# The FFN weight blocks of a two-layer decoder: loads, high parts and low parts tied to one order on three queues

## The chip, the cores and the metric

The kernel runs on one core of one Trainium2 chip. A core has engines that run side by side, each with a queue of its own: TensorE (PE in the profile; PEld is its weight load), VectorE (DVE), ScalarE (ACT), GpSimd (POOL) and SyncE (SP), which here only issues DMA transfers. The metric is the device time of one execution in microseconds, as a median over runs.

## The reference: what is computed

Two layers work on 528 tokens (16 learned meta tokens and 512 real ones) of width 1024. Each layer has a mixer sub-layer (attention heads, a convolution group and a short gated convolution that read one projection) and an FFN sub-layer. The change touches the FFN alone:

```python
u = rms_norm(h, pre_g)
z = jnp.einsum("bld,df->blf", u, w_up)          # 1024 -> 2 * 2816
z = causal_depthwise_conv(z, conv_w)            # 3 taps along the tokens
g, up = jnp.split(z, 2, axis=-1)
y = jnp.einsum("blf,fd->bld", jax.nn.silu(g) * up, w_down)   # 2816 -> 1024
return h + rms_norm(y, post_g)
```

All of it is float32.

## The kernel before, in words

**Three products for one.** TensorE runs in its fast float32 format, which keeps fewer bits. So each operand is split in a high part (a rounded copy) and a low part (the rest), and a product is made of high by high, high by low and low by high. A weight block takes three steps before TensorE can use it: a load from memory into a `raw` tile (issued by SP), the high part by a copy with a cast on ACT (tile `whi`), and the low part by a subtraction on DVE (tile `wlo`).

**Blocks and their order.** `chunk_list` writes down all weight blocks in the order in which they are used. In the FFN the 22 column pairs f (a gate block and an up block of 1024 x 128 each) come in three parts of 8, 7 and 7; behind each part come eight blocks of the down projection. `next_w` takes the next block that is ready and has `prep_one` issue the three steps for blocks further on, so that two are ahead.

**Pairs with seven products.** For the f in `SEVEN` (15 to 20 in the first layer; 8 to 13 and 15 to 20 in the second) `seven_pair` uses a scheme of Strassen's kind: seven block products in the place of eight, on sums of weight blocks that other code has stored in `w_sum`. `prep_one` then makes four blocks of a pair: the gate block (g below; lines 646, 648, 649) and three parts "c", "b" and "d" (lines 630, 638, 639). `seven_pair` calls for them as g, c, b, d. The products run g, c, then the d of the pair before (kept back in `late_ups`), then b, g, c, b.

**Buffers.** g and c go to `whi` and `wlo`, three buffers each; b goes to `shi` and `slo`, one buffer each; d goes to the tiles of `y_pair(7)`, one buffer. `raw` has three buffers; in parts 1 and 2, while pairs with seven products are still to come, four places in the tile of h serve too (`spare_tile`), in a fixed round of seven, save while `down_sum` uses them.

**What sets the order of instructions.** In the mixers and at the ends of the sub-layers (`manual_schedule`) a planner in the kernel (`Flow`) writes the order out. Elsewhere, so in the bulk of the FFNs, a scheduler at build time sets the order on each engine: of the instructions that could start by its estimates it takes the one that was written first. An instruction that was written later can go ahead of an earlier one that has to wait for a buffer. `tc.issue_after(ins)` adds one rule: what is written inside it and runs on the same engine as `ins` is issued behind `ins`. It makes no wait between engines.

**Other users of these orders.** `last_load` and `last_low` hold the last load and the last subtraction. The copies of `sum_steps` and the reload of h at the end of the last pair are issued behind `last_load`; the steps of `down_sum` behind `last_low`. Before the change `last_load` isn't set by the loads of parts c, b and d. The down products' results are copied out of PSUM at line 2403 (part 0, ACT) and added at line 2405 (part 1, DVE).

Of the kernel before, what the change touches and what calls it, by code (L numbers as in the profile page):

```python
# [10 lines left out]
F32 = mybir.dt.float32  # L11
# [5 lines left out]
P = 128  # L17
# [100 lines left out]
def chunk_cols(c):  # L118
    return sum(n for _, n in c[4])
# [254 lines left out]
def stt_us(n):  # L374
    return 0.22 + 0.00102 * n
# [13 lines left out]
def tile_hybrid_trunk(ctx: ExitStack, tc: tile.TileContext, xT, wflat, pv_d, out):  # L389
    nc = tc.nc  # L390
# [3 lines left out]
    def T(pool, shape, dt, tag, bufs=None):  # L394
        uid[0] += 1
        kw = {} if bufs is None else {"bufs": bufs}
        return pool.tile(list(shape), dt, tag=tag, name=f"{tag}_{uid[0]}", **kw)
# [89 lines left out]
    def half_sl(hf):  # L487
        return slice(H * hf, H * (hf + 1))
# [15 lines left out]
    offs = []  # L504
# [15 lines left out]
    def flat_w(i):  # L520

        n = chunks[i][3] * chunk_cols(chunks[i])
        return wflat[offs[i]:offs[i] + P * n].rearrange("(p s) -> p s", p=P)
# [32 lines left out]
    def wtile(i, tag):  # L556
        if chunks[i][0] == "a_pw_w":
            if tag == "whi":
                pw_place[0] = pw_place[0]()
            n = chunks[i][3] * chunk_cols(chunks[i])  # L560
            return pw_place[0][:, :n] if tag == "whi" else pw_place[0][:, n:2 * n]
        return T(wx[0], [P, WCHUNK], F32R, tag) if i in wide else T(wp, [P, CHUNK], F32R, tag)

    parts, last_load, last_low = deque(), [None], [None]
    spare, n_raw = [None], [0]

    def spare_tile(j):
# [3 lines left out]
    def raw_tile():  # L571

        if spare[0] is not None and not in_spare[0]:
            j = (None, 0, None, 1, None, 2, 3)[n_raw[0] % 7]
            n_raw[0] += 1
            if j is not None:
                return spare_tile(j)
        return T(wp, [P, CHUNK], F32, "raw", 3)
# [39 lines left out]
    def prep_one():  # L618
        i = wpos[0]
        if i >= len(chunks):  # L620
            return
        if i in seven_up:
            if not parts:
                t = sums[seven_up[i]]
                parts.extend((("c", t[:, 1::2]), ("b", t[:, 0:3:2]), ("d", flat_w(i)[:, SB:])))
            kind, src = parts.popleft()
            wpos[0] += not parts
            raw = raw_tile()
            sz = SB if kind == "d" else 2 * SB
            nc.sync.dma_start(raw[:, :sz] if kind == "d" else raw[:, :sz].rearrange("p (e s) -> p e s", e=2),  # L630
                              src)
            if kind == "b":
                hi, lo = (T(tx[0], [P, 2 * SB], F32R, t) for t in ("shi", "slo"))
            elif kind == "c":
                hi, lo = (T(wp, [P, CHUNK], F32R, t) for t in ("whi", "wlo"))
            else:
                hi, lo = y_pair(max(PARTS) - 1)
            nc.scalar.copy(hi[:, :sz], raw[:, :sz])
            last_low[0] = nc.vector.tensor_sub(lo[:, :sz], raw[:, :sz], hi[:, :sz].bitcast(F32))
            ready.append((i, tuple(t[:, :sz].rearrange("p (k n) -> p k n", n=P) for t in (hi, lo))))  # L640
            return
        wpos[0] += 1
        kn, n = chunks[i][3], chunk_cols(chunks[i])
        sz = kn * n
        raw = raw_tile()
        last_load[0] = nc.sync.dma_start(raw[:, :sz], wflat[offs[i]:offs[i] + P * sz].rearrange("(p s) -> p s", p=P))
        hi, lo = wtile(i, "whi"), wtile(i, "wlo")
        nc.scalar.copy(hi[:, :sz], raw[:, :sz])  # L648
        last_low[0] = nc.vector.tensor_sub(lo[:, :sz], raw[:, :sz], hi[:, :sz].bitcast(F32))  # L649
        ready.append((i, tuple(t[:, :sz].rearrange("p (k n) -> p k n", n=n) for t in (hi, lo))))  # L650

    to_store = deque(i for i, c in enumerate(chunks) if c[1] == 1 and c[0] == "w_in" and MASK[sum(d[:2] == c[:2] for d in chunks[:i])] == "1")
# [21 lines left out]
    def prefetch(n):  # L674

        while wpos[0] < len(chunks):
            if wpos[0] not in wide and sum(i not in wide for i, _ in ready) >= n:
                return
            prep_one()
# [8 lines left out]
    def dve(us, fn, *after, **kw):  # L688
        return flow.op("dve", us, fn, after, **kw)
# [152 lines left out]
    def two(t):  # L842
        return t.rearrange("p (a b) -> p a b", a=2)
# [1172 lines left out]
    def y_pair(i):  # L2016
        t = T(ypool, [P, 2, L], F32R, f"y{i}")
        return t[:, 0], t[:, 1]
# [6 lines left out]
    with tc.tile_pool(name="pre", bufs=2, reuse_waits="tile") as sp, tc.manual_schedule(engines=every):  # L2025
# [13 lines left out]
        for k in range(KD):  # L2039
            hk, hi, lo, gc = h[:, k, :H], u_raw[0][k], u_raw[1][k], g0[:, k:k + 1]  # L2040
            c = act(act_us(H) + 0.06, lambda hk=hk, hi=hi, gc=gc: nc.scalar.activation(hi, hk, AF.Copy, scale=gc),
                    h_at[0, k - k % 2], prio=0)
            d = dve(stt_us(H), lambda hk=hk, hi=hi, lo=lo, gc=gc: nc.vector.scalar_tensor_tensor(
                lo, in0=hk, scalar=gc, in1=hi.bitcast(F32), op0=ALU.mult, op1=ALU.subtract), c, prio=0)
# [45 lines left out]
    for l in range(DEPTH):  # L2090
# [23 lines left out]
        with tc.tile_pool(name=f"fp{l}", bufs=2, reuse_waits="tile") as fp:  # L2114
# [223 lines left out]
            for part, nf in enumerate(PARTS):  # L2338
# [41 lines left out]
                if part < len(PARTS) - 1:  # L2380
# [3 lines left out]
                    for some in ((0, 1), *((m,) for m in range(2, KD))):  # L2384
# [12 lines left out]
                        for m, ps in zip(some, tiles):  # L2397
                            if final:
                                d, src = yp[:, m, t0:], ps[:, 0, :2 * fw]
                            else:  # L2400
                                d, src = two(yp[:, m, t0:]), ps[:, :, :fw]
# [7 lines left out]
                else:  # L2409
# [7 lines left out]
                    if not final:  # L2417
                        raw = list(zip(*[g[f0 + k] for k in range(nf)], y_pair(nf)))
                        raw = [[[t[:, half_sl(hf)] for t in ts] for ts in raw] if hf < 2 else None for hf in range(2)]
# [64 lines left out]
```

## Time and profile before

| | us |
|---|---|
| median of 3 runs | 1271.03 (1269.31 to 1271.58) |
| the profiled execution | 1270.68 |
| its span | 1269.0 |
| PE busy | 1249.8 (98%) |
| DVE busy | 920.9 (73%) |
| ACT busy | 705.2 (56%) |

The span is the time between the first and the last instruction of the profiled execution; its own time is a little longer. L646 is line 646 of the kernel. SPq is SP's DMA queue. In a row of waits stand the total, the count and the longest. In a timeline row stand the start and the length in us, the engine, the line, the operation and its tiles, and in square brackets how long the engine sat idle before it and who ended that.

### The profile page before, as it was taken

The page shows a single profiled execution, that of the slowest core. Times are in us where ns is not written, and L with a number is a line of the kernel's source. Part 1 is how long each engine was busy: PE and PEld are TensorE (multiplying, and loading weights), DVE is VectorE, ACT ScalarE, POOL GpSimd, SP SyncE. Part 2 cuts the span into 40 slices and gives each one's busy share as a digit, 9 for nine tenths or more (in the row PEclk, how much of TensorE's full clock was granted, in tenths as well). Part 3 has the DMA queues.
Part 4 walks back from the last instruction along what each step waited for, and adds up shares of the span by engine and source line. Part 5 has one row for each costly group of instructions (what it writes and reads, how often), then busy time and mean ns, then how long its engine had stood idle before and what let it go on. Part 6 is the DMA issues. An engine that isn't in the chain of part 4 may idle for free.

```text
span 1269.0 us, 24272 instructions
## 1 busy us (share of the span) xinstructions
PE 1249.8 (98%) x9590; PEld 1198.2 (94%) x9590; DVE 920.9 (73%) x1569; ACT 705.2 (56%) x1365; POOL 162.0 (13%) x343
## 2 busy tenths in 40 slices
PE   8999999999999999999999999999999999999997
PEld 8998898999999999999999988999999799979996
DVE  7887866589874665587688878656799748756954
ACT  7254576654444643476673545775554447526763
POOL 1324311001101100000003244110021000000000
PEclk9999999999999999999999999999999999999999
DMA  7257231726558634544552584547166655475611
GB/s 243 81 155 175 72 102 53 249 86 151 182 164 313 212 112 142 205 165 144 192 205 61 159 191 113 143 118 233 70 166 184 172 176 169 152 241 160 202 61 67
DMA packets 76146, 197.93 MB, mean 156 GB/s; under 512 B 8240, under 2 KB 18608, under 8 KB 75520
## 3 DMA queue, kind: packets, MB, share of 16 engines
q1 hardware_dynamic: 64048, 162.69, 40.0%
q0 software_dynamic: 11984, 33.69, 11.1%
q8 instruction: 75, 1.23, 0.4%
q14 instruction: 39, 0.32, 0.1%
HBM read 162.17 MB, written 44.30 MB: 163 GB/s over the span
## 4 chain that ended last, share of the span: by engine, by line
PE 66%; DVE 2%; ACT 1%; issue 0%; DMA 0%; POOL 0%; DVEq 0%; ACTq 0%
PE psum L833 45%; PE psum L2281 14%; PE psum L1403 2%; PE psum L1667 2%; PE psum L970 1%; PE psum L1633 1%; PE psum L1589 0%; DMA h<-w_sum 0%; DVE yp L1046 0%; PE psum L1733 0%; PE psum L1319 0%; DVE h L1056 0%; POOL dm L1604 0%; DVE ulo L1064 0%; DVE wlo L649 0%
## 5 line engine op out<-in xcount | busy, mean ns | idle before, releaser
L833 PE MATMUL psum<-y,whi 128*128 128x264 f32 (+3 forms) x1968 | 384.7, 299 | 2.7 <-ACT yp L2403 1.4
L833 PEld LDWEIGHTS psum<-y,whi 128*128 128x128 f32 x1968 | 305.1, 188 | 17.2 <-ACT yp L2403 2.6
L833 PE MATMUL psum<-uhi,whi 128*128 128x264 f32 (+1 forms) x1264 | 310.3, 288 | 1.6 <-ACT uhi L2065 0.8
L833 PE MATMUL psum<-ulo,whi 128*128 128x264 f32 (+1 forms) x1264 | 304.1, 284 | 0.6 <-DVE ulo L2067 0.4
L833 PE MATMUL psum<-uhi,wlo 128*128 128x264 f32 (+1 forms) x1264 | 303.2, 284 | 0.0
L833 PE MATMUL psum<-y,wlo 128*128 128x264 f32 (+3 forms) x984 | 273.9, 297 | 1.1 <-DVE wlo L789 1.1
L833 PEld LDWEIGHTS psum<-uhi,whi 128*128 128x128 f32 x1264 | 216.0, 188 | 5.9 <-issue 1.6
L833 PEld LDWEIGHTS psum<-ulo,whi 128*128 128x128 f32 x1264 | 216.1, 188 | 1.3 <-DVE ulo L2067 0.6
L833 PEld LDWEIGHTS psum<-uhi,wlo 128*128 128x128 f32 x1264 | 215.6, 188 | 0.0
L833 PEld LDWEIGHTS psum<-y,wlo 128*128 128x128 f32 x984 | 177.6, 188 | 6.7 <-DVE wlo L789 1.6
L2169 DVE SCALAR_TENSOR_TENSOR c<-zs,pv,c 128x528 f32<-128x528 f32 (+1 forms) x176 | 130.9, 757 | 18.4 <-ACT c L2167 16.4
L648 ACT CAST whi<-raw 128x1024 fp32r<-128x1024 f32 (+1 forms) x67 | 68.2, 1021 | 98.4 <-PE psum L833 72.6
L789 DVE TENSOR_TENSOR wlo<-raw,whi 128x1024 fp32r<-128x1024 f32 (+2 forms) x80 | 95.4, 1203 | 29.8 <-ACT whi L785 29.5
L649 DVE TENSOR_TENSOR wlo<-raw,whi 128x1024 fp32r<-128x1024 f32 (+1 forms) x67 | 79.4, 1185 | 28.1 <-ACT whi L648 28.0
L785 ACT CAST whi<-raw 128x1024 fp32r<-128x1024 f32 (+2 forms) x80 | 81.7, 1031 | 24.9 <-PE psum L833 18.0
L1149 DVE SCALAR_TENSOR_TENSOR cacc<-apad,pv,cacc 128x528 f32<-128x528 f32 x120 | 87.7, 772 | 0.1
L2167 ACT ACTIVATE c<-zs,pv 128x528 f32<-128x528 f32 (+1 forms) x88 | 63.1, 727 | 7.0 <-DVE zs L2132 2.7
L2281 PE MATMUL psum<-uhi,whi 128*128 128x258 f32 (+1 forms) x216 | 61.2, 284 | 0.0
L2281 PE MATMUL psum<-ulo,whi 128*128 128x258 f32 (+1 forms) x216 | 61.0, 283 | 0.0
L2281 PE MATMUL psum<-uhi,wlo 128*128 128x258 f32 (+1 forms) x216 | 60.5, 282 | 0.0
L2281 PE MATMUL psum<-t,shi 128*128 128x258 f32 (+1 forms) x288 | 54.2, 283 | 0.0
L1667 PE MATMUL psum<-pf,vals 128*128 128x400 f32 (+3 forms) x160 | 50.7, 399 | 0.6 <-POOL pf L1647 0.6
(273 smaller groups left out, 2193.2 us busy)
## 6 DMA issues: line engine op xcount, KB each, us to landing
raw<-in_w_dram SPq DMA_DIRECT2D x115, 512.0 KB, 4.5
h<-in_w_dram SPq DMA_DIRECT2D x27, 512.0 KB, 4.8
raw<-in_w_dram SPq DMA_DIRECT2D x30, 448.0 KB, 5.1
raw<-w_sum SPq DMA_DIRECT2D x18, 512.0 KB, 5.1
h<-w_sum SPq DMA_DIRECT2D x18, 512.0 KB, 5.4
h<-in_w_dram POOLq DMA_DIRECT2D x16, 512.0 KB, 3.8
w_sum<-h POOLq DMA_DIRECT2D x16, 512.0 KB, 5.3
w_sum<-in_w_dram SPq DMA_DIRECT2D x20, 256.0 KB, 5.0
```

The lines of the kernel that those rows point to most:

```text
L648: nc.scalar.copy(hi[:, :sz], raw[:, :sz])
L649: last_low[0] = nc.vector.tensor_sub(lo[:, :sz], raw[:, :sz], hi[:, :sz].bitcast(F32))
L785: nc.scalar.copy(box["hi"][:, :sz], box["raw"][:, :sz])
L789: nc.vector.tensor_sub(lo[:, :sz], box["raw"][:, :sz], box["hi"][:, :sz].bitcast(F32))
L833: nc.tensor.matmul(d, lhsT=w[a][:, k, cols], rhs=rhs(b, k, hf), start=start and i == 0 and p == 0, stop=stop and i == n - 1 and p == 2)
L970: nc.tensor.matmul(ps, lhsT=om_d, rhs=box["c"][:, i, :], start=j + i == 0, stop=j + 1 == n_parts and i == tiles[-1])
L1149: nc.vector.scalar_tensor_tensor(conv[j], in0=src, in1=conv[j], scalar=col("a_dw_w", CK * j + i), op0=ALU.mult, op1=ALU.add)
L1403: nc.tensor.matmul(ps[:n, :nw], lhsT=(uhi, ulo)[ui][:, k, P * b:P * b + n], rhs=w[wi][:, k % 4, :], start=k == 0 and p == 0, stop=k == KD ...
L1667: nc.tensor.matmul(acc[:, s0 - qa:qz - qa], lhsT=vals[:, b].rearrange("p h d -> p (h d)")[:, o:o + P], rhs=box["p"], start=b == 0, stop=b ...
L2167: nc.scalar.activation(dst, src[:, 2:2 + 2 * fw], AF.Copy, scale=wtap(2, t))
L2169: nc.vector.scalar_tensor_tensor(dst, in0=src[:, i:i + 2 * fw], scalar=wtap(i, t), in1=dst, op0=ALU.mult, op1=ALU.add)
L2281: nc.tensor.matmul(psum[:, bank, :n7], lhsT=w[a][:, k0 + k, :], rhs=rhs(b, k), start=start and k == 0 and p == 0, stop=stop and k == K2 - ...
```

## The change

A new helper, `split_next`, issues the three steps of a block. Each of them is issued behind the same step of the block before: the load behind the last load on SP, the high part behind the last high part on ACT, the low part behind the last low part on DVE. Both branches of `prep_one` call it, for whole blocks and for the parts c, b and d. The blocks that the planner issues (`plan_block`) and those of `store_one` are as before.

```diff
-    parts, last_load, last_low = deque(), [None], [None]
+    parts, last_load, last_low, last_high = deque(), [None], [None], [None]
+
+    def split_next(raw, src, hi, lo, sz):
+
+        with ExitStack() as order:
+            for last in (last_load, last_high, last_low):
+                if last[0] is not None:
+                    order.enter_context(tc.issue_after(last[0].ins))
+            last_load[0] = nc.sync.dma_start(raw, src)
+            flat = raw if raw.ndim == 2 else raw.rearrange("p e s -> p (e s)")
+            last_high[0] = nc.scalar.copy(hi[:, :sz], flat)
+            last_low[0] = nc.vector.tensor_sub(lo[:, :sz], flat, hi[:, :sz].bitcast(F32))
...
             sz = SB if kind == "d" else 2 * SB
-            nc.sync.dma_start(raw[:, :sz] if kind == "d" else raw[:, :sz].rearrange("p (e s) -> p e s", e=2),
-                              src)
...
-            nc.scalar.copy(hi[:, :sz], raw[:, :sz])
-            last_low[0] = nc.vector.tensor_sub(lo[:, :sz], raw[:, :sz], hi[:, :sz].bitcast(F32))
+            split_next(raw[:, :sz] if kind == "d" else raw[:, :sz].rearrange("p (e s) -> p e s", e=2), src, hi, lo, sz)
...
-        last_load[0] = nc.sync.dma_start(raw[:, :sz], wflat[offs[i]:offs[i] + P * sz].rearrange("(p s) -> p s", p=P))
         hi, lo = wtile(i, "whi"), wtile(i, "wlo")
-        nc.scalar.copy(hi[:, :sz], raw[:, :sz])
-        last_low[0] = nc.vector.tensor_sub(lo[:, :sz], raw[:, :sz], hi[:, :sz].bitcast(F32))
+        split_next(raw[:, :sz], wflat[offs[i]:offs[i] + P * sz].rearrange("(p s) -> p s", p=P), hi, lo, sz)
```

## The prediction

> **What bounds the kernel now.** I read the page first: its busy shares and its row of the granted clock.
>
> ```profile
> PE 1249.8 (98%) x9590; PEld 1198.2 (94%) x9590; DVE 920.9 (73%) x1569; ACT 705.2 (56%) x1365; POOL 162.0 (13%) x343
> ...
> PEclk9999999999999999999999999999999999999999
> ```
>
> TensorE is busy for 98% of the span at a full clock, and no other engine is above 73%. The change touches only the FFNs' weight blocks, so the next view is the busy time by stretch, asked once over the first layer's FFN (250 to 607 us) and once over the second's (905 to 1225 us). Columns: stretch, its length, then busy us and count of PE, PEld, DVE, ACT, POOL, then clock, DMA share and GB/s. The two rows that begin with "sum" stand for all stretches of a layer.
>
> ```profile
> 365.00:380.00 15.00, 14.54 (x120) 14.33 (x119) 12.54 (x16) 8.55 (x13) 1.15 (x2) 1.00 0.66 224
> ...
> sum 357.00, PE 356.47 PEld 355.66 DVE 256.95 ACT 185.98 POOL 25.59; mean PE 23.76 PEld 23.71 DVE 17.13 ACT 12.40 POOL 1.71
> ```
>
> ```profile
> 905.00:915.00 10.00, 9.12 (x68) 8.49 (x68) 5.12 (x13) 2.79 (x6) 0.00 (x0) 1.00 0.27 110
> ...
> 985.00:1000.00 15.00, 14.03 (x61) 11.01 (x60) 10.14 (x14) 6.42 (x10) 1.85 (x3) 1.00 0.36 88
> ...
> 1060.00:1070.00 10.00, 10.00 (x86) 10.00 (x84) 8.97 (x12) 7.54 (x14) 0.00 (x0) 1.00 0.44 146
> ...
> 1112.00:1142.00 30.00, 29.69 (x128) 23.77 (x127) 18.78 (x24) 7.92 (x9) 2.14 (x4) 1.00 0.75 254
> ...
> sum 320.00, PE 317.69 PEld 299.53 DVE 237.75 ACT 173.53 POOL 21.18; mean PE 15.13 PEld 14.26 DVE 11.32 ACT 8.26 POOL 1.01
> ```
>
> TensorE's idle time in the two FFNs is 357.00 - 356.47 = 0.53 us and 320.00 - 317.69 = 2.31 us. Of the latter, 0.88 us lies in 905 to 915, where the order is still the written-out one. What the change can win is therefore at most 0.53 + 2.31 - 0.88 = 1.96 us. [...]
>
> Third, the waits, for what ended the idle time of PE:
>
> ```profile
> PE psum L1613 <- POOL dm L1604: 2.0, 2, 1.0
> PE psum L833 <- ACT yp L2403: 1.4, 2, 1.0
> ...
> PE psum L833 <- DVE wlo L789: 1.1, 2, 0.7
> ...
> PE psum L833 <- DVE yp L2405: 0.3, 1, 0.3
> ```
>
> No row names the lines that split the FFNs' blocks in this part of the kernel (638, 639, 648, 649). The wait on wlo is at L789, which the change doesn't touch. What is left is the copy-out of a down projection's first PSUM tile, at L2403 and L2405. The chain of waits at the largest of them shows why it is late:
>
> ```profile
> 984.50 10.02 PE psum L833 x43
> 994.52 0.03 ACTq L648
> 994.54 0.04 issue
> 994.58 1.05 ACT whi L648
> ```
>
> A cast of a weight block started on ACT at 994.58, just ahead of the copy, and held it for 1.05 us.
>
> **Does the change do something?** The blocks in question are those of an FFN column pair with seven products: a gate block (g, L648), a block c (whi at L638), a block b (shi) and a block d (y). TensorE's program takes them g, c, b, d, pair after pair. On ACT, in layer 1:
>
> ```profile
> 1045.00 0.62 ACT L638 CAST y<-h 128x512 fp32r<-128x512 f32 x1 [1.04 <-PE psum L2281]
> ...
> 1047.75 1.05 ACT L638 CAST whi<-h 128x1024 fp32r<-128x1024 f32 x1 [0.53 <-PE psum L2281]
> ...
> 1049.18 1.05 ACT L648 CAST whi<-h 128x1024 fp32r<-128x1024 f32 x1
> ...
> 1051.11 1.05 ACT L638 CAST shi<-raw 128x1024 fp32r<-128x1024 f32 x1 [0.36 <-PE psum L2281]
> ...
> 1052.93 1.05 ACT L638 CAST whi<-raw 128x1024 fp32r<-128x1024 f32 x1
> ...
> 1056.74 0.62 ACT L638 CAST y<-h 128x512 fp32r<-128x512 f32 x1 [2.21 <-PE psum L2281]
> ...
> 1059.28 1.05 ACT L648 CAST whi<-h 128x1024 fp32r<-128x1024 f32 x1
> ```
>
> In TensorE's order one g, one c and one b stand between two d's. Here, between the d's of 1045.00 and 1056.74, there are c, g, b, c: the second c, and the g before it, belong to the pair after. So g and c of the next pair overtake b and d of this one. With the change the order is c, b, d, g, c: the g of 1049.18 has to follow the d of 1056.74. The change is real, and it mostly delays blocks that came early.
>
> **The change part by part.**
>
> *Work.* No instruction is added or removed; the edges bind only the issue order on one engine each, so they add no wait between engines. Busy time: 0.
>
> *Loads on SP.* A load is now held by the load before it. The queue waits for buffers already:
>
> ```profile
> SPq L646 <- DVE wlo L649: 240.7, 49, 22.8
> ...
> SPq L630 <- DVE wlo L649: 41.1, 19, 5.4
> ```
>
> ```profile
> raw<-in_w_dram SPq DMA_DIRECT2D x115, 512.0 KB, 4.5
> ...
> h<-w_sum SPq DMA_DIRECT2D x18, 512.0 KB, 5.4
> ```
>
> A load lands 4.5 to 5.4 us after issue. The raw buffers go round in sevens (three of their own, four in the spare tile), four blocks to a pair, and a pair's seven products take 7 x 1.45 = 10.2 us (a product of twelve matmuls: the d product below runs from 1055.09 to the next row's 1056.54). A buffer comes round every 7/4 x 10.2 = 17.8 us; less 5.4 for landing and about 2.3 for cast and low part, some 10 us of lead are left. Cost: 0. That cover is gone at the ends of parts, where the spare tile is lent to the sums and three buffers are left. There, in layer 1, TensorE spends 21 to 24 matmuls on a down block, at 29.69 / 128 = 0.232 us each (1112 to 1142), 4.9 us at the least, so a buffer comes round every 14.6 us, against the 7.7 that load and split take: again 0. The bound above is one landing, 5.4 us, at an end of a part.
>
> *Casts and low parts.* Here lies the price. The rows of TensorE and DVE that belong to it:
>
> ```profile
> 1052.68 0.35 ACT L2321 COPY zs<-psum 128x256 f32<-128x256 f32 x1
> ```
>
> ```profile
> 1055.09 1.62 PE L2281 MATMUL psum<-t,y 128*128 128x258 f32 x12
> 1056.54 0.28 PE L2281 MATMUL psum<-t,slo 128*128 128x258 f32 x1
> ...
> 1059.20 0.41 PE L2281 MATMUL psum<-t,whi 128*128 128x258 f32 x2
> ```
>
> ```profile
> 1050.33 1.22 DVE L649 TENSOR_TENSOR wlo<-h,whi 128x1024 fp32r<-128x1024 f32 x1
> ...
> 1053.33 0.74 DVE L2169 SCALAR_TENSOR_TENSOR c<-zs,pv,c 128x512 f32<-128x512 f32 x1
> ```
>
> The cast of d has one buffer (y7), so it starts only when the product with the d before it is done (1056.54, cast at 1056.74). Behind it now stands the next g: 0.2 + 0.62 + 1.05 + 1.22 = 3.1 us from the end of a d product to a g whose low part is there. In program order four products lie between (b, g, c, b): 4 x 1.45 = 5.8 us. Bare slack: 2.7 us, where g had been ready since 1050.33 + 1.22 = 1051.55, some 6 us ahead of use (the c product at 1059.20 stands for the pair's start; g is one product earlier, 1057.75). Next late is c of the same pair. It waits for the buffer of the pair before (three whi buffers), free two products before that pair's end, and is wanted one product after it: 3 x 1.45 = 4.35 us against 0.2 + 1.05 + 1.22 = 2.5. Slack 1.9 us, and b likewise (free at the pair's end, wanted three products later).
>
> From these slacks the queues take their part. DVE is busy for 8.97 of 10 us in this stretch and ACT for 7.54; one operation ahead on each (0.35 to 1.05 on ACT, 0.74 to 1.22 on DVE) costs 1.1 to 2.3 us. With the small end every slack holds and the cost is 0. With the large end c and b are short by 2.3 - 1.9 = 0.4 us a pair. But TensorE's own order gives here: in this trace the d product ran at 1055.09, though the copy that it waits for ended at 1052.68 + 0.35 = 1053.03, and it can go first where g isn't there. There are 6 + 6 + 6 = 18 such pairs. So the bounds are 0 and 18 x 0.4 = 7.2 us. I take 0.05 us a pair, 0.9 us in all, near the lower end, because the lower end is the nominal queue and a product of 1.45 us can be exchanged for a late one. A gain is possible only from the copy-outs: 1.4 + 0.3 = 1.7 us. The cast that caused the largest (L648 at 994.58) stands among down blocks that are already in order, so I take 0 of it.
>
> *Elsewhere.* In part 0 of both FFNs the raw ring has three buffers and the order is the natural one; nothing moves. The copies for the sums and the reload of h now also stand behind the loads of parts c, b, d on SP; both are wanted tens of us later, cost 0.
>
> *Sum.* The profiled execution took 1270.68 us: a span of 1269.0 and 1.7 around it. 1270.68 + 0 - 0 + 0.9 = 1271.6; it lies 0.35 under the median of the runs shown (1271.03), so the forecast is 1271.9 us, which can't be told from no change (0.2%, 2.5 us, is about what a measurement of this kernel resolves).
>
> **The rivals.**
>
> *A cast of d that waits holds the whole split queue (slower).* Place: ACT between the d cast and the next g, in the 18 pairs. It decides once the operations ahead on ACT and DVE exceed the slack of 1.9 us. The row of 1056.74 speaks for it: ACT stood idle for 2.21 us before that cast, and now everything split later stands behind it. Against it: TensorE lost nothing to that idle time, and has other products. Price: 0.3 us a pair (between 0.14, where 2.5 us are reached, and 0.4) is 5.4 us: 1276.4 us. [...]
>
> *The copy-outs become free (faster).* If all casts move away from the first copy of each down projection, 1.7 us go, 1.96 at most: 1269.1 to 1269.3 us. For it: one cast is shown in front of one copy. Against it: those casts don't change places. Even whole it stays inside 0.2%; more than 2.5 us would need something that no row shows.
>
> *Loads too late (slower).* At an end of a part a load into the spare tile waits for the store of the sums and now holds the loads behind it. One landing exposed, 5.4 us: 1276.4 us. Against it: SP's waits are long already (22.8 us at the most) and no PE wait names a DMA.
>
> *It changes nothing at all:* the order is already there. The ACT rows above speak against it, but the time would be the same: 1271.0 us.
>
> **How the numbers follow.** Forecast (0 to 2 us more): 0.50. No effect at all: 0.10. The waiting cast: 0.24. Loads too late: 0.06. Copy-outs free: 0.10, of which 0.08 for a gain over 0.2%, by a reordering that I can't see. So faster 0.08, the same 0.50 + 0.10 + 0.02 = 0.62, slower 0.24 + 0.06 = 0.30. The range: below, the ceiling of 1.96 us with no cost, 1269.1; above, the waiting cast at its price, 1276.4, and up to 0.4 us a pair, 1271.0 + 7.2 = 1278.2, of which I keep 1277.0. The likeliest case alone spans 1270 to 1273.
>
> **What would show it.** The casts run b, d, g, c in each pair, and the low parts alike. The idle time of PE in 1030 to 1102, 1142 to 1210 and 524 to 596, 0.00 now, stays under 1 us in all; a row "PE psum L2281 <- DVE" or "<- ACT whi" of several us would be the waiting cast, "<- DMA" the loads. L2403 stays near 1.4 us. I am wrong if PE's idle time in the FFNs rises by over 2.5 us, or if the time falls under 1268.5, which the idle time in these rows can't pay for.

## The result, and the profile after

The changed kernel takes 1273.09 us (median of 12 runs, 1272.04 to 1274.37) against 1270.36 us before (12 runs, 1268.60 to 1271.64). The ratio is 1.0022, with a 95% interval of 1.0015 to 1.0030: about 2.7 us slower. The time lies in the predicted range; the forecast was 1271.9 us, 1.2 us less.

No work came or went: DVE is busy for 920.2 us after (920.9 before), ACT for 705.0 (705.2), and TensorE runs the same 9590 matmuls. The waits of PE that the prediction watched don't show the loss either. The copy-out is as before:

```profile
PE psum L839 <- ACT yp L2409: 1.4, 2, 1.0
```

(Lines are six further down after the change: 2403 is now 2409, 2281 is 2287. Loads, casts and subtractions of the FFNs' blocks now have lines 572, 574 and 575, those of the helper.)

What shows the loss is the count of matmuls in a fixed time. Here are three stretches inside the pairs with seven products, before and then after. The second number is the busy time of PE, and in brackets behind it stands the count of matmuls that ran in the stretch (two or three of each count began just ahead of it).

```profile
545.00:575.00 30.00, 30.00 (x249) 30.00 (x249) 25.77 (x34) 22.80 (x41) 0.00 (x0) 1.00 0.56 180
1050.00:1080.00 30.00, 30.00 (x252) 30.00 (x252) 25.77 (x35) 22.38 (x42) 0.54 (x1) 1.00 0.55 174
1162.00:1202.00 40.00, 40.00 (x335) 40.00 (x334) 34.95 (x47) 30.49 (x55) 0.00 (x0) 1.00 0.62 193
```

```profile
545.00:575.00 30.00, 30.00 (x242) 29.41 (x241) 24.09 (x33) 22.63 (x40) 0.00 (x0) 1.00 0.55 176
1050.00:1080.00 30.00, 29.96 (x244) 29.29 (x243) 24.00 (x34) 22.36 (x40) 0.00 (x0) 1.00 0.51 163
1162.00:1202.00 40.00, 39.96 (x327) 39.29 (x326) 32.37 (x45) 29.73 (x54) 0.00 (x0) 1.00 0.53 173
```

Before, the three counts add up to 836 matmuls in 100 us, so one takes about 0.12 us. After, they add up to 813: 23 fewer, or some 2.75 us, which is about the whole loss. The busy time of PE hides it: it is still 99.92 of 100 us, because a matmul is listed as 0.28 us long while the next one starts 0.12 us behind it, so that a step of 0.28 us leaves no gap. The column behind it, the weight loads, shows more: 97.99 us after the change, where it was 100.00. And the waits of the weight loads name the place; before the change no such row is there:

```profile
PEld psum L2287 <- ACT whi L574: 1.9, 9, 0.2
```

One such stall, on TensorE after the change (start, length, line, operation):

```profile
1068.86 0.28 PE L2287 MATMUL psum<-uhi,whi 128*128 128x258 f32 x1
1068.99 0.28 PE L2287 MATMUL psum<-ulo,whi 128*128 128x258 f32 x1
1069.27 0.50 PE L2287 MATMUL psum<-t,whi 128*128 128x258 f32 x2
1069.61 0.36 PE L2287 MATMUL psum<-uhi,wlo 128*128 128x258 f32 x1
1069.82 0.28 PE L2287 MATMUL psum<-uhi,whi 128*128 128x258 f32 x1
```

From start to start an unhindered matmul takes 0.12 us (100 / 836 above). Here the steps are 0.28 to the first matmul of c, 0.34 for the two of c, and 0.21: (0.28 - 0.12) + (0.34 - 0.24) + (0.21 - 0.12) = 0.35 us. This pattern stands at nine pairs, the fourth to the sixth in each of the three blocks of six, and costs 0.31 to 0.39 us at each, 3.1 us in all. And what ACT did meanwhile:

```profile
1066.43 0.62 ACT L574 CAST y<-raw 128x512 fp32r<-128x512 f32 x1 [0.35 <-PE psum L2287]
1066.96 0.37 ACT L2333 COPY zs<-psum 128x258 f32<-128x258 f32 x1
1067.22 1.05 ACT L574 CAST whi<-h 128x1024 fp32r<-128x1024 f32 x1
1068.17 1.04 ACT L574 CAST whi<-raw 128x1024 fp32r<-128x1024 f32 x1
1069.12 0.72 ACT L2173 ACTIVATE c<-zs,pv 128x512 f32<-128x512 f32 x1
```

d, a copy, g, c, one right behind the other: d's cast could start only when the d product before it was done, and c's cast ended at 1068.17 + 1.04 = 1069.21, just before TensorE's start at 1069.27.

In TensorE's order, 24 matmuls lie between the end of that d product and the first two of c, which stand well ahead of the rest of their product. In the third pair of each block 60 matmuls lie there, the five products of program order (b, g, c, b and the next g), and in the first two pairs no d product of the block comes before c. Those pairs lose nothing.

A part of the old cost went, too. Before, on ACT and then on PE, shortly ahead of the first pair with seven products of the second layer:

```profile
1010.22 1.05 ACT L638 CAST shi<-h 128x1024 fp32r<-128x1024 f32 x1 [5.33 <-DMA h<-w_sum]
...
1011.69 1.05 ACT L648 CAST whi<-raw 128x1024 fp32r<-128x1024 f32 x1
1012.64 0.58 ACT L2403 COPY yp<-psum 128x512 f32<-128x512 f32 x1
```

```profile
1012.80 0.40 PE L833 MATMUL psum<-y,wlo 128*128 128x512 f32 x1
1013.27 0.50 PE L833 MATMUL psum<-y,whi 128*128 128x512 f32 x1
```

A cast of b, well ahead of its turn, had ACT stand for 5.33 us until its data had landed; the copy-out behind it came late, and TensorE lost 0.47 - 0.23 = 0.24 us there (0.23 us is the usual step of the down products' matmuls, 29.69 / 128 from 1112 to 1142 us) and some 0.1 us behind it. After the change this gap isn't there. At the first c of that layer, near 1032, another 0.2 us went, and near 1225 a new stall of 0.25 us came: 3.1 - 0.35 - 0.2 + 0.25 = 2.8 us, against 2.73 us between the medians.

### The profile page after: what moved, and what is told of

Its sections match the earlier page's. It is cut to its first block, busy times and chain, and to the rows that moved or that the text cites. A ratio compares the mean times of both kernels' runs of the same rounds, so it can differ in the third digit from the quotient of the medians.

```text
span 1271.9 us, 24282 instructions
## 1 busy us (share of the span) xinstructions
PE 1252.6 (98%) x9590; PEld 1199.1 (94%) x9590; DVE 920.2 (72%) x1569; ACT 705.0 (55%) x1365; POOL 160.3 (13%) x343
## 5 line engine op out<-in xcount | busy, mean ns | idle before, releaser
L574 ACT CAST whi<-raw 128x1024 fp32r<-128x1024 f32 (+1 forms) x76 | 77.7, 1025 | 125.1 <-PE psum L839 99.4
L575 DVE TENSOR_TENSOR wlo<-raw,whi 128x1024 fp32r<-128x1024 f32 (+1 forms) x76 | 90.4, 1189 | 46.7 <-ACT whi L574 44.0
L575 DVE TENSOR_TENSOR wlo<-h,whi 128x1024 fp32r<-128x1024 f32 (+1 forms) x34 | 41.3, 1214 | 33.1 <-ACT whi L574 32.8
```

The costliest lines, as they stand in the source:

```text
L574: last_high[0] = nc.scalar.copy(hi[:, :sz], flat)
L575: last_low[0] = nc.vector.tensor_sub(lo[:, :sz], flat, hi[:, :sz].bitcast(F32))
```

## The experiments

Theory A: the cast of d waits for d's one buffer, and since g and c of the next pair now stand behind it on ACT, c comes late. Theory B: the order of the low parts on DVE does it. Theory C: the order of the loads on SP does it. Each run was timed in five rounds against the kernel before on the same chip.

**One order at a time.** Three kernels keep one of the three edges of the helper each:

```diff
-            for last in (last_load, last_high, last_low):
+            for last in (last_high,):
```

The other two have `(last_low,)` and `(last_load,)` in this place.

> Only the casts on ACT keep the order; loads and low parts are free. Theory A (the cast of d waits for its single buffer and the next pair's g and c stand behind it on ACT): the loss is all here, +2.7 us over before (ratio 1.002), with the same small gaps on PE before the c product of nine pairs, about 0.37 us each. Theory B (the low parts' order on DVE does it) and theory C (the loads' order on SP does it): no loss, ratio 1.000.

> Only the low parts on DVE keep the order. Theory A: g and c are cast early again, but their low parts still stand behind the low part of d, so a part of the loss stays: 0.1 to 0.2 us in nine pairs, +1 to +2 us (ratio 1.001). Theory B: all of it, +2.7 us. Theory C: none, ratio 1.000.

> Only the loads on SP keep the order. Theories A and B: no loss, ratio 1.000, no gap on PE within the pairs. Theory C: +2.7 us, and the casts of c would wait for their data.

| kept | median us | ratio to before (95%) |
|---|---|---|
| casts | 1272.66 | 1.0022 (1.0013 to 1.0031) |
| low parts | 1270.05 | 0.9999 (0.9990 to 1.0008) |
| loads | 1269.30 | 0.9997 (0.9988 to 1.0006) |

With the casts in order, then the low parts, then the loads, the stretch from 1050 to 1080 us:

```profile
1050.00:1080.00 30.00, 29.93 (x244) 29.26 (x243) 24.03 (x33) 22.49 (x40) 0.00 (x0) 1.00 0.55 174
```

```profile
1050.00:1080.00 30.00, 30.00 (x252) 30.00 (x251) 26.73 (x38) 23.34 (x42) 0.00 (x0) 1.00 0.59 187
```

```profile
1050.00:1080.00 30.00, 30.00 (x252) 30.00 (x251) 25.73 (x35) 22.73 (x43) 0.53 (x1) 1.00 0.50 169
```

The casts' order alone costs what the change costs: 244 matmuls in this stretch, as there. B and C fall. The gap near 1013 is gone in all three, so any one of the orders is enough for that. Theory A's own figure for the low parts (1 to 2 us) was too high; ordering them alone costs nothing that can be measured.

**d out of the order.** The helper gets a flag; with it, d neither waits for the last block nor becomes the last block:

```diff
+            for last in () if free else (last_load, last_high, last_low):
...
+            if not free:
+                last_load[0], last_high[0], last_low[0] = load, high, low
```

> All three orders are kept, save that part d takes no place in them: it neither follows nor is followed. Theory A: the loss is gone, ratio 1.000 (within 0.5 us of before), no gaps of PE within the pairs. A rival to it within ACT (part b, with one buffer too, holds the queue as much as d): the loss stays, +2.7 us.

It took 1277.79 us, ratio 1.0058 (1.0046 to 1.0071): neither theory's number, and the loss is far larger. ACT and then PE of this kernel:

```profile
1065.18 1.05 ACT L574 CAST shi<-h 128x1024 fp32r<-128x1024 f32 x1 [0.45 <-PE psum L2289]
1066.13 1.04 ACT L574 CAST whi<-h 128x1024 fp32r<-128x1024 f32 x1
1067.08 0.37 ACT L2329 COPY zs<-psum 128x256 f32<-128x256 f32 x1
```

```profile
1065.10 0.28 PE L2289 MATMUL psum<-uhi,wlo 128*128 128x258 f32 x1
...
1066.54 0.29 PE L2289 MATMUL psum<-t,wlo 128*128 128x258 f32 x1
1067.22 0.39 PE L2289 MATMUL psum<-uhi,whi 128*128 128x258 f32 x1 [0.40 <-ACT whi L574]
```

Now g stands right behind b, which has one buffer too. Between the end of the b product and the first matmul of the next g, TensorE had 13 matmuls in its issue order: 13 x 0.12 = 1.56 us from 1065.10. The two casts end at 1066.13 + 1.04 = 1067.17. TensorE waits from 1066.66 on, about 0.56 us. The d product can't fill this: it adds to the PSUM tile that the copy of 1067.08 reads, and this copy stands behind the same two casts. So the two theories of this run were both too simple: what counts here is the chain of casts behind a part with one buffer, against the matmuls that the issue order holds between that buffer's release and the first use. Why this build holds only 13 there was not tried.

**A second buffer for d.** If A is right, the change with two buffers for d must lose nothing; by what the run before taught, b could take its place:

```diff
-                hi, lo = y_pair(max(PARTS) - 1)
+                n_d[0] += 1
+                hi, lo = y_pair(max(PARTS) - 1 - (n_d[0] + 1) % 2)
```

> The changed kernel with a second buffer for part d (the tiles y6 and y7 in turn). Theory A as it stood (d's cast waits for d's one buffer and holds g and c behind it): the loss is gone, ratio 1.000. Theory A2, after the run that left d out of the order and lost 7.4 us (any cast that waits for a buffer and stands ahead of the next g holds it; b is the next one): a loss stays, 2 to 8 us, with PE waiting for casts of whi in nine pairs.

1269.98 us, ratio 0.9994 (0.9985 to 1.0003): the loss is gone, with all three orders kept. In the stretch, and on ACT:

```profile
1050.00:1080.00 30.00, 30.00 (x253) 30.00 (x252) 26.51 (x36) 23.41 (x43) 0.48 (x1) 1.00 0.57 189
```

```profile
1059.66 1.05 ACT L574 CAST shi<-h 128x1024 fp32r<-128x1024 f32 x1
1060.62 0.61 ACT L574 CAST y<-raw 128x512 fp32r<-128x512 f32 x1
...
1061.40 1.05 ACT L574 CAST whi<-h 128x1024 fp32r<-128x1024 f32 x1
```

d's cast now follows b's at once and waits for no product. The result is A's; A2's loss did not come.

**The order of use.** The change issues a pair's blocks as g, c, b, d, but the products run g, c, d of the pair before, b. This kernel keeps all three orders and makes the blocks in the order of the products:

```diff
-                parts.extend((("c", t[:, 1::2]), ("b", t[:, 0:3:2]), ("d", flat_w(i)[:, SB:])))
+                parts.extend((("c", t[:, 1::2]), *held_d, ("b", t[:, 0:3:2])))
+                held_d[:] = [("d", flat_w(i)[:, SB:])]
+                if i + 2 not in seven_up:
+                    parts.extend(held_d)
+                    held_d.clear()
...
-                wd = next_w()
                 def rest():
+                    wd = next_w()
```

> All three orders are kept, but the blocks are made in the order in which the products run: g, c, then d of the pair before, then b; d of the last pair comes last. Theory A: d's cast no longer stands ahead of the next g and c, so the loss is gone: ratio 1.000, perhaps 0.4 us less than before. If order itself costs (any fixed order takes away the freedom to go ahead): the loss stays at +2.7 us or near it.

1269.75 us against 1269.72 before, ratio 1.0001 (0.9992 to 1.0010). The loss is gone; a gain of 0.4 us can't be told from nothing. On ACT, d stands behind a c, and g behind b:

```profile
1056.05 1.05 ACT L574 CAST whi<-h 128x1024 fp32r<-128x1024 f32 x1 [0.93 <-PE psum L2293]
1057.00 0.62 ACT L574 CAST y<-raw 128x512 fp32r<-128x512 f32 x1
...
1058.95 1.05 ACT L574 CAST shi<-h 128x1024 fp32r<-128x1024 f32 x1 [0.54 <-PE psum L2293]
1059.91 1.05 ACT L574 CAST whi<-raw 128x1024 fp32r<-128x1024 f32 x1
```

g stands behind b here as in the run with d out of the order, but TensorE has more to do after b's release:

```profile
1058.87 0.28 PE L2293 MATMUL psum<-uhi,wlo 128*128 128x258 f32 x1
...
1061.51 0.28 PE L2293 MATMUL psum<-uhi,whi 128*128 128x258 f32 x1
```

(1061.51 - 1058.87) / 0.12 = 22 matmuls lie before the next g, and the casts end at 1059.91 + 1.05 = 1060.96, ahead of them. So a fixed order as such costs nothing.

One thing these two runs leave open. TensorE's own order is not that of the changed kernel in them: from the third pair of a block on, 60 matmuls (two buffers) and 58 (order of use) lie between the end of a d product and the next c, where the changed kernel has 24 in the pairs that lose. They took away the wait of d's cast ahead of g and c, and c's early place as well; which of the two alone would have been enough is not shown. The run with the casts alone in order loses as the changed kernel does, and has its 24.

**The copy-out behind a cast.** The prediction left one thing on the table: the copy-out that a cast holds up. The kernel before, with the first of these copies on DVE:

```diff
+                            if part == 0 and m == 0:
+                                evac = glo_ins[0] = nc.vector.tensor_copy(d, src)
-                            if part == 0:
+                            elif part == 0:
```

> The kernel before, with one edit: the copy-out of the first block of the down projection's part 0 runs on DVE in place of ACT, in both layers. If the cast ahead of that copy on ACT is what PE waits for there (0.46 and 0.97 us before), both waits shrink to some 0.2 us: 1.0 to 1.5 us less than before (ratio 0.999). If DVE is as occupied at that moment, or its copy out of PSUM is slower than ACT's 0.48 us, nothing changes, ratio 1.000.

1272.94 us, ratio 1.0027 (1.0016 to 1.0039): slower, though one of its six runs took only 1270.88 us. ACT near 1011 us, the wait of PE, and then the stretches around it (the value behind POOL's is the granted clock):

```profile
1011.45 1.05 ACT L638 CAST shi<-h 128x1024 fp32r<-128x1024 f32 x1 [8.03 <-DMA h<-w_sum]
...
1013.87 0.57 ACT L2405 COPY yp<-psum 128x512 f32<-128x512 f32 x1
```

```profile
PE psum L833 <- ACT yp L2405: 2.8, 1, 2.8
```

```profile
1010.00:1013.00 3.00, 1.73 (x8) 1.07 (x6) 0.47 (x1) 1.55 (x3) 0.00 (x0) 1.00 1.04 391
1013.00:1016.00 3.00, 1.50 (x6) 1.21 (x7) 3.00 (x4) 3.00 (x5) 0.00 (x0) 0.92 0.50 181
1016.00:1019.00 3.00, 3.00 (x9) 2.37 (x8) 2.97 (x4) 0.83 (x2) 0.53 (x1) 0.52 0.81 275
1019.00:1022.00 3.00, 3.00 (x15) 2.41 (x14) 0.00 (x0) 0.28 (x1) 0.00 (x0) 1.00 0.90 318
```

The early cast of b, which cost a third of a microsecond before, now comes after 8.03 us of waiting for its data, and TensorE waits for the copy-out behind it for 2.8 us. Why the data landed later was not looked into. Then the granted clock is 0.52 for 3 us: 9 matmuls ran there, and 15 in the next 3 us at a clock of 1.00. At some 0.23 us each, the six missing ones are an estimated 1.4 us more.

**Both together.** In the order of use, that cast should not come early:

> The order of use (g, c, d of the pair before, b) and the first copy-out of part 0 on DVE together. If in the run with that copy alone the 2.9 us stall came from an early cast of b that waited for its data on ACT: in order it cannot come early, the stall is gone, and what the copy and the order save stays: 0.7 us near 365, 0.65 us near 995 and 0.4 us near 1013, 1.8 us in all, ratio 0.9986. If the copy on DVE is itself the cause: still some 3 us slower, ratio 1.002 to 1.003.

1269.07 us against 1270.33, ratio 0.9989 (0.9980 to 0.9998): the stall at 1011 is gone, and the sum is the fastest version here, just clear of the kernel before and 0.3% under the changed one. The gain is 1.3 us; the expected 1.8 lie inside the interval. In the profiled execution a later copy-out, still on ACT, has a wait of its own, behind a cast that waited for its data:

```profile
PE psum L845 <- ACT yp L2417: 0.7, 1, 0.7
```

```profile
380.26 1.05 ACT L674 CAST shi<-h 128x1024 fp32r<-128x1024 f32 x1 [6.40 <-DMA h<-in_w_dram]
```

But this execution was the slowest of the eleven (1270.07 us), and the next kernel's profile lacks that wait at the same median. So the wait is not shown to belong to the kernel.

With, on top of it, two columns in place of one left for the end of the first two down blocks (`for group in (ks[:-2], ks[-2:])`):

> The kernel with order of use and the copy on DVE, and the first two down blocks leave their last two columns for the end in place of the last one, so that 6 or 12 matmuls lie behind the first block's last matmul and not 3 or 6. If the wait there is the time of one copy-out less those matmuls: the waits near 493, 995 and 1112 go too (0.35, 0.6 and 0.6 us), 3.3 us less than before in all, ratio 0.9974. If the last columns aren't ready that early: PE waits for y there, and the gain stays at 1.8 us or less.

1269.10 us, ratio 0.9990 (0.9981 to 0.9998). No further gain, and the expected 3.3 us were not had. Of the waits named, only that near 493 shrank, by 0.1 us; in the second layer the wait for the first copy-out, near 995, is the same with the edit and without it:

```profile
PE psum L845 <- DVE yp L2415: 0.3, 1, 0.3
```

Why it stayed there was not followed up.

## Why the prediction was right and where it failed

The time lies in the range, but what came was not the likeliest case. The medians are 2.73 us apart, three times the 0.9 us of the sum, and the interval (1.0015 to 1.0030) is clear of 1, where the forecast was one that can't be told from no change. What came is the rival of the waiting cast, which had a chance of 0.24, at about half its price of 5.4 us. The range held because that price was inside it.

*The ceiling and the work.* That little could be won, and that nothing was added, held: 9590 matmuls as before, and no version here gains more than 1.3 us.

*The order.* As read from the casts before: d now stands ahead of the next g and c, on ACT.

*Loads, 0.* Right: the loads' order alone gives 0.9997.

*Casts and low parts, 0.05 us a pair.* This is the term that failed, by its size. Nine pairs lose 3.1 us, 0.34 us each on average, where 0.9 us in all were put. Two steps in it were wrong. The slack of c was reckoned from the release of its own buffer, 1.9 us; in truth c's cast ran behind d, a copy and g, so its clock started at the end of the d product (1066.23) and it was done 2.98 us later, at 1069.21. TensorE had 24 matmuls in that time and not the 60 of program order, 24 x 0.12 = 2.88 us, and so was at c at about 1069.11: a slack of -0.1 us and not 1.9. And "a product of 1.45 us can be exchanged for a late one" did not hold. The order was set when the kernel was built, and TensorE stood before c's first matmul until 1069.27, though the matmul of uhi and whi at 1069.82, two places behind c's, reads a high part of g that had been there since 1067.22 + 1.05 = 1068.27. That the scheduler's estimates had c ready in time is likely, but not shown.

*The waiting cast.* The rival's mechanism was right, and so were its place (what came late was c, behind that g) and its price of 0.3 us a pair. The count was not: the first three pairs of each block don't pay, so it is 9 and not 18. That the order of the low parts would take part did not show: it costs nothing alone.

*Copy-outs, no gain.* The large one stayed (1.4 us in the waits, before and after), as argued. But a small one near 1013 went, some 0.35 us that the prediction didn't see: the copy-out behind the early cast of b that waited for its data.

*What would show it.* I had said that the idle time of PE would tell. It rose by only 0.08 us in these 100 us, so the bound of 2.5 us on it could not have caught the loss. The count of matmuls told, and so did the waits of the weight loads, which were not among the signs.

## What to carry to other kernels

A fixed order on an engine is only as good as its match with the order of use and with the buffers: in this kernel, a second buffer for the part that waited, or another place for it in the order, took the loss away (ratios of 0.9994 and 1.0001, where the change has 1.0022). Before an order is pinned, add up the operations from the release of that buffer to the end of the last one that stands behind it, and count the matmuls that TensorE has in the same time. And where TensorE is the bound, compare counts of matmuls in equal stretches (here 836 and 813 in 100 us) and the waits of the weight loads (here a new row of 1.9 us), not the busy time of PE (here 100.00 and 99.92 us).

## What the runs showed of the hardware that was not expected

The stall at 1069 cost more than its length. The first matmul of c starts 0.16 us late, and the steps behind it are 0.10 and 0.09 us longer than usual: 0.35 us for a wait of 0.16.

Behind a stall of about 3 us the clock fell as well: in the run with the copy-out on DVE, the granted clock was 0.92 from 1013 to 1016 us, where the wait of 2.8 us ends, 0.52 from 1016 to 1019 us, and 1.00 again in the next 3 us. The kernel before has a clock of 1.00 from 1013 to 1019 us, and 15 matmuls from 1016 to 1019 us where that run has 9. That the stall brought the fall is a reading of one profiled execution; no run tried it apart.
